# Attention: the division by the sums on GpSimd, the second copy of the turned probabilities on VectorE, four heads ahead, a finished tile's bank released one step later

## The chip, the cores and the metric

The program runs on one core of a Trainium2 chip. The metric is the device time of one execution in microseconds (us); the kernel before has a median of 1674.59 us over 3 runs (1673.91 to 1675.4). Engine names are those of the profile: PE multiplies matrices (PEld loads its weights), DVE is VectorE, ACT is ScalarE, POOL is GpSimd, SP issues most of the DMAs.

## The reference, cut to what matters

Two layers of a backbone over 512 latent tokens and 256 context tokens, width 1024. The change lies in the mixer of layer 0, which puts two groups of heads side by side:

```python
def _softmax_attend(q, k, v):
    s = jnp.einsum('bhgqd,bhkd->bhgqk', q, k, preferred_element_type=jnp.float32) * (ATT_HEAD_DIM ** -0.5)
    p = jax.nn.softmax(s, axis=-1).astype(v.dtype)
    return jnp.einsum('bhgqk,bhkd->bhgqd', p, v)

def _gated_readout(o, og, gain):
    return _merge(_rms(o, gain) * jax.nn.silu(og))

    # in _even_mixer, for the latent tokens
    a_lat = _gated_readout(dirs[0][1] + dirs[1][1], og[:, :, n_ctx:], gla_out_norm)   # 4 gated-linear heads of width 128
    o_blocks = lax.map(lambda qb: _softmax_attend(qb, k_all, va), q_blocks)           # 8 attention heads of width 64
    o_lat = jnp.concatenate([a_lat, b_lat], axis=-1)                                  # then one output projection
```

A latent query reads 768 keys (512 latent, 256 context); a context query reads the 256 context keys.

## The kernel before

**The stage.** `even_mixer` runs generators in a written order (`run("...")`): each letter takes one step of one generator. `x` is `Attention.context()`, `y` is `Attention.latent()`, `t` turns the gated heads into the projection's input (`gated_T`), `r0` and `r1` are the readouts of the two halves of the gated heads, `M` computes modulation columns. While `self.pinned` is set, PE's instructions keep this program order; what the other engines do is put in order by the framework's scheduler, and each engine then executes its own list strictly in that order.

**One latent step.** There are 4 tiles of 128 queries and 8 heads, so 32 pairs (tile, head), numbered i = 0 to 31. Step i of `latent` computes S(i), the scores of pair i (128x768, two banks, tile `S`, two of them in all); DVE takes the row maximum (`amx`, L193), ACT the exponential with its row sum (`prob`, L195), DVE the reciprocal of the sum (`ars`, L196) and the division, as a product of 128x768 in place (L198). The same step then turns an older pair j = i - `ahead` on PE (`turned`: six 128x128 transposes `pT`, four into a bank of the tag `tr`, two into a bank of the tag `sc0` or `sc1`). The four are copied to SBUF by ACT (`probT`, 128x512), the two (128x256) by ACT too, or for every fourth pair by DVE (L210). Of every second step, `values` multiplies two turned pairs with the values (`attO`, 24 small matmuls), and behind the eighth pair of a tile `done` has the result `attO` copied out by ACT (L763) and DVE (L764).

**The bank of the second part.** A tile t of `attO` lives in the bank `sc0` or `sc1` (t % 2). `other()` names the bank in which the two late transposes go: the one that the running tile doesn't hold, or, once that tile is in `self.ended`, the one that it held. Two pairs in succession use the same bank, so the two late transposes of a pair can start only when the copy of the pair before has read it.

**Order in the list of steps.** The latent generator takes its first five steps among those of the context attention; the loop at L1271 takes the rest, with `behind` putting one step of `t`, `r1` or `M` behind some of them. Every fourth pair of a tile (i % 8 = 4) is followed by `queries` for the next tile: four transposes `qT`, read by ACT and by DVE.

**Readout.** `readout(c)` squares (ACT), sums (DVE), takes the power -1/2 (`rstd`, POOL, tile `rs`), multiplies the heads by it (L1233) and by the gate (L1235, with 0.5 where the gate was made by tanh).

Of the kernel before, what the change touches and what calls it, by code (L numbers as in the profile page):

```python
# [17 lines left out]
P = 128  # L18
# [9 lines left out]
EPS = 1e-6  # L28
# [105 lines left out]
class Attention:  # L134
# [43 lines left out]
    def scores(self, t, heads, p):  # L178

        nc, net = self.nc, self.net  # L180
        s = net.mm_tile("S")
        nk = p.shape[-1]
        w = 1024 // len(heads)
        for x, hd in enumerate(heads):
            at = w * x
            for ks in self.k[int(t >= LT)]:
                m = ks[0].shape[-1]
                for i, k in enumerate(ks):
                    net.mm(s[:, at : at + m], self.q[t][:, hd, :], k[:, hd // 4, :], start=(i == 0), stop=(i == 1))
                at += m  # L190
        sv = s.rearrange("p (x k) -> p x k", k=w)[:, :, :nk]
        mx, sm, r = (net.sm.tile([P, len(heads)], F32, tag=tag, name=tag) for tag in (("amx", "asm", "ars") if len(heads) == 1 else ("ms4", "ss4", "rs4")))
        nc.vector.tensor_reduce(mx, sv, axis=AX.X, op=ALU.min)  # L193
        for x in range(len(heads)):
            nc.scalar.activation(p[:, x, :], sv[:, x, :], AF.Exp, bias=mx[:, x : x + 1], scale=-1.0, accum_out=sm[:, x : x + 1])  # L195
        nc.vector.reciprocal(r, sm)  # L196
        for x in range(len(heads)):
            nc.vector.tensor_scalar(p[:, x, :], p[:, x, :], r[:, x : x + 1], None, op0=ALU.mult)  # L198

# [29 lines left out]
                )  # L229

    def done(self, t):
        self.ended.append(t)
        self.net.put(self.cat, slice(4, 8), slice(t * P, (t + 1) * P), self.po[t].rearrange("p (j i) -> p j i", j=4))

    def context(self):
        wp = self.net.wp
        wide = lambda tag, name, dt=F32R: wp.tile([P, WU], dt, tag=tag, bufs=4, name=name)
        kc = wide("wH", "kc").rearrange("p (x n i) -> p x n i", x=2, n=2)
        self.k[1] = [(kc[:, 0], kc[:, 1])]
        ps, pTs = {}, {}  # L240

        def queries(t, tag):
            self.queries(t, wide(tag, f"qs{t}").rearrange("p (h i) -> p h i", h=8))

        def scores(b):
            ps[b] = wp.tile([P, WU], F32, tag="raw", bufs=3, name=f"prob{b}")
            self.scores(LT + b // 2, range(4 * (b % 2), 4 * (b % 2) + 4), ps[b].rearrange("p (x k) -> p x k", x=4))

        def turned(b):
            pTs[b] = wide("wL", f"probT{b}", F32).rearrange("p (c i) -> p c i", c=8)  # L250
            self.turned(ps.pop(b), pTs[b], (1,))

        def values(b):
            pT = pTs.pop(b)
            for j in range(2):
                self.values(LT + b // 2, 2 * (b % 2) + j, [pT[:, 2 * x : 2 * x + 2, :] for x in (2 * j, 2 * j + 1)])

        self.keys(LT, NTT - LT, self.k[1][0])
        queries(LT, "wH")
        yield  # L260
        queries(LT + 1, "wL")
        scores(0)
        yield
        scores(1)
        yield
        turned(0)
        yield
        scores(2)
        values(0)
        yield  # L270
        scores(3)
        turned(1)
        yield
        values(1)
        yield
        self.done(LT)
        turned(2)
        yield
        values(2)
        turned(3)  # L280
        yield
        values(3)
        self.done(LT + 1)

    def latent(self, ap):
        kl = [ap.tile([P, 2, SEQ], F32R, name=f"k{x}") for x in "HL"]
        self.k[0] = [kl] + self.k[1]
        q = lambda t: ap.tile([P, 8, P], F32R, tag="qs", bufs=2, name=f"qs{t}")
        self.keys(0, LT, kl)
        yield  # L290
        self.queries(0, q(0))
        yield

        ahead = 3
        ps, pTs, due = {}, {}, []
        for i in range(8 * LT + ahead + 2):
            t, hd = divmod(i, 8)
            if t < LT:
                ps[i] = ap.tile([P, NT], F32, tag="prob", bufs=4, name="prob")
                self.scores(t, (hd,), ps[i][:, None, :])  # L300
            j = i - ahead
            if 0 <= j < 8 * LT:
                pTs[j] = ap.tile([P, NTT, P], F32, tag="probT", bufs=4, name="probT")
                self.turned(ps.pop(j), pTs[j], (1,) if j % 4 == 3 else (), self.other())
            if due:
                t0, n, xs = due.pop()
                self.values(t0, n, xs)
                if n == 3:
                    self.done(t0)
            if 0 <= j < 8 * LT and j % 2:  # L310
                due.append((j // 8, j // 2 % 4, [pTs.pop(x) for x in (j - 1, j)]))
            if t + 1 < LT and hd == 4:
                self.queries(t + 1, q(t + 1))
            yield


class Net:
# [360 lines left out]
        return gv  # L678


    def rstd(self, ss, n, w=1):
        nc = self.nc
        ms = self.sm.tile([P, w], F32, tag=f"ms{w}", name="ms")
        nc.vector.tensor_scalar(ms, ss, 1.0 / n, EPS, op0=ALU.mult, op1=ALU.add)  # L684
        rs = self.sm.tile([P, w], F32, tag=f"rs{w}", name="rs")
        nc.gpsimd.tensor_tensor(rs, ms, self.neghalf.to_broadcast([P, w]), op=ALU.pow)  # L686
        return rs
# [427 lines left out]
    def even_mixer(self, h, mix, z):  # L1115
# [106 lines left out]
        def readout(c, tiles=tiles):  # L1222

            for t0 in tiles:
                cs = slice(256 * c, 256 * c + 256)
                o = gv[:, t0 : t0 + 2, cs].rearrange("p t (h v) -> p t h v", h=2)
                sq = self.wp.tile([P, WU], F32, tag="mraw", bufs=2, name="sq")[:, :512]
                nc.scalar.activation(sq.rearrange("p (t n) -> p t n", t=2), gv[:, t0 : t0 + 2, cs], AF.Square)
                ss = self.sm.tile([P, 4], F32, tag="ss4", name="ss4")
                nc.vector.tensor_reduce(ss, sq.rearrange("p (x v) -> p x v", v=P), axis=AX.X, op=ALU.add)  # L1230
                rs = self.rstd(ss, P, 4)
                rb = rs.rearrange("p (t h) -> p t h", t=2)[:, :, :, None].to_broadcast([P, 2, 2, P])
                nc.vector.tensor_tensor(o, o, rb, op=ALU.mult)  # L1233
                x = gv[:, t0 : t0 + 2, cs]
                nc.vector.scalar_tensor_tensor(x, x, 0.5 if c else 1.0, og[c][:, t0 : t0 + 2, :], op0=ALU.mult, op1=ALU.mult)  # L1235


        kinds = {
# [28 lines left out]
        with self.pool("att") as ap:  # L1267
            run("y x y g1 x y x y M x y")

            behind = {6: "t", 7: "r1", 9: "t", 10: "r1", 14: "M", 15: "r1", 16: "M", 17: "t", 19: "t", 22: "t", 24: "t", 26: "t", 29: "t"}  # L1270
            for i in range(3, 32 + 5):  # L1271
                run("y " + behind.get(i, ""))
        self.pinned = False
        return cat
# [1010 lines left out]
```

## Time and profile before

| | us |
|---|---|
| median of the runs | 1674.59 |
| the profiled execution | 1675.78 |
| its span | 1674.0 |
| PE busy (share of the span) | 1644.8 (98%) |
| DVE busy | 1311.1 (78%) |
| ACT busy | 916.1 (55%) |
| POOL busy | 129.4 (8%) |

The span is what the trace covers of the profiled execution; 1.8 us lie around it. A matmul's end is modelled, so that in a row the times of matmuls overlap: what PE needed for a group is read from its start to the start of the next one. The latent attention is the stretch from about 250 to 342 us.

### The profile page before, as it was taken

Reading aid. Unit: us, or ns where it says so; the run is one execution under the profiler, and the core shown is the slowest. Engines: PE = TensorE matmul, PEld = TensorE weight load, DVE = VectorE, ACT = ScalarE, POOL = GpSimd, SP = SyncE. Lnnn points to the kernel's source line nnn. Section 1 sums busy time; section 2 is a strip of 40 time slices with the busy share of each in tenths; the row PEclk is TensorE's granted clock in tenths of the full one; section 3 lists DMA queues with packets and bytes.
Section 4 is the critical chain, followed back from the end, with each engine's and each line's share of the span. In section 5 each row is a group of like instructions: output and inputs, shape, how many; then the busy total and the mean of one; then the engine's idle time right before and its main releaser. Section 6 shows DMA issues by size and latency. Waiting matters only on the chain.

```text
span 1674.0 us, 32524 instructions
## 1 busy us (share of the span) xinstructions
PE 1644.8 (98%) x13407; PEld 1481.1 (88%) x13407; DVE 1311.1 (78%) x2097; ACT 916.1 (55%) x1551; POOL 129.4 (8%) x139
## 2 busy tenths in 40 slices
PE   9999999999999999999999999999999999999998
PEld 7899987888999999998887888888888899999886
DVE  5999678976898988777668648788775599987887
ACT  5745567845544443446447436666664565555664
POOL 2004110011000000002102000000000100000310
PEclk9999999999999999999999999999999999999999
DMA  9641012164243445249525541121124333333973
GB/s 336 213 132 41 3 45 86 50 227 160 80 126 114 139 151 176 78 153 205 100 84 193 200 127 57 48 65 40 51 65 150 126 114 115 114 101 102 226 164 138
DMA packets 184736, 204.79 MB, mean 122 GB/s; under 512 B 7142, under 2 KB 141836, under 8 KB 184588
## 3 DMA queue, kind: packets, MB, share of 16 engines
q1 hardware_dynamic: 173996, 181.98, 34.7%
q0 software_dynamic: 9024, 17.30, 5.9%
q10 hardware_dynamic: 1568, 3.43, 0.6%
q8 instruction: 105, 1.72, 0.4%
q14 instruction: 43, 0.35, 0.1%
HBM read 193.23 MB, written 9.46 MB: 121 GB/s over the span
## 4 chain that ended last, share of the span: by engine, by line
PE 83%; DVE 8%; ACT 3%; DMA 3%; issue 2%; POOL 0%; SPq 0%; DVEq 0%; ACTq 0%; POOLq 0%
PE nat L355 12%; PE a L355 10%; PE ff L355 8%; PE E L355 7%; PE oproj L355 6%; PE x L355 6%; PE o L355 5%; PE D L355 4%; PE b L355 3%; PE fq L355 3%; PE gqk L355 2%; PE pearly L355 2%; PE q L355 2%; PE S L355 2%; PE poh L355 1%
## 5 line engine op out<-in xcount | busy, mean ns | idle before, releaser
L355 PE MATMUL nat<-wH,x 128*128 128x256 f32 (+2 forms) x968 | 226.7, 322 | 1.2 <-ACT x L2014 0.6
L860 ACT CAST wH<-raw 128x1024 fp32r<-128x1024 f32 x120 | 124.8, 1051 | 102.7 <-DVE raw L885 40.7
L355 PEld LDWEIGHTS nat<-wH,x 128*128 128x128 f32 x968 | 161.9, 190 | 19.5 <-ACT natq L1196 1.7
L861 DVE TENSOR_TENSOR wL<-raw,wH 128x1024 fp32r<-128x1024 f32 x120 | 145.7, 1222 | 23.6 <-ACT wH L860 23.3
L355 PE MATMUL nat<-wL,x 128*128 128x256 f32 (+2 forms) x484 | 153.5, 317 | 1.8 <-DVE wL L804 1.8
L804 DVE TENSOR_TENSOR wL<-raw,wH 128x1024 fp32r<-128x1024 f32 x79 | 95.8, 1222 | 50.6 <-ACT wH L803 49.8
L355 PE MATMUL ff<-x,wH 128*128 128x512 f32 (+1 forms) x512 | 127.6, 340 | 0.0
L686 POOL TENSOR_TENSOR rs<-ms,neghalf 128x1 f32<-128x1 f32 (+2 forms) x56 | 60.1, 1076 | 777.7 <-DVE ms L684 777.6
L803 ACT CAST wH<-raw 128x1024 fp32r<-128x1024 f32 x79 | 82.2, 1050 | 68.5 <-PE ff L355 19.7
L355 PE MATMUL oproj<-wH,x 128*128 128x512 f32 x320 | 102.2, 394 | 0.4 <-ACT x L1330 0.4
L355 PEld LDWEIGHTS nat<-wL,x 128*128 128x128 f32 x484 | 92.1, 190 | 7.8 <-DVE wL L804 2.7
L615 DVE SCALAR_TENSOR_TENSOR macc<-mraw,scT,macc 128x1024 f32<-128x1024 f32 x70 | 88.0, 1282 | 11.6 <-DMA mraw<-in_mod_w_dram 11.4
L355 PEld LDWEIGHTS ff<-x,wH 128*128 128x128 f32 x512 | 87.3, 190 | 10.0
L355 PE MATMUL x<-wH,two 128*128 128x512 f32 x280 | 90.5, 392 | 0.9 <-DVE y L1851 0.7
L1773 POOL DMA_DIRECT2D t<-in_ffn_w_down_dram x36 | 41.9, 1200 | 640.1 <-DVE t L1812 338.3
L1012 ACT COPY qkh<-arr 128x512 f32<-128x512 f32 x112 | 70.2, 641 | 36.6 <-DVE arr L1017 32.3
L355 PE MATMUL ff<-x,wL 128*128 128x256 f32 (+1 forms) x256 | 86.2, 337 | 0.0
L885 DVE TENSOR_TENSOR raw<-raw 128x512 f32<-128x512 f32 x120 | 82.8, 690 | 2.8
L1017 DVE TENSOR_TENSOR arr<-arr,f 128x512 f32<-128x512 f32 x112 | 74.4, 688 | 2.0 <-ACT qkh L1012 0.3
L355 PEld LDWEIGHTS oproj<-wH,x 128*128 128x128 f32 x320 | 59.9, 188 | 13.0 <-ACT x L1330 1.0
L355 PE MATMUL a<-T,wH 128*128 128x384 f32 (+1 forms) x320 | 70.5, 309 | 0.6 <-ACT qb L923 0.5
L355 PE MATMUL E<-T,wH 128*128 128x384 f32 (+1 forms) x320 | 70.4, 309 | 0.7 <-DVE go L938 0.7
(425 smaller groups left out, 4558.6 us busy)
## 6 DMA issues: line engine op xcount, KB each, us to landing
mraw<-in_mod_w_dram SPq DMA_DIRECT2D x80, 512.0 KB, 4.4
raw<-in_ffn_w_gate_dram SPq DMA_DIRECT2D x44, 512.0 KB, 3.9
raw<-in_ffn_w_up_dram SPq DMA_DIRECT2D x44, 512.0 KB, 4.9
raw<-in_odd_w_in_dram SPq DMA_DIRECT2D x40, 512.0 KB, 3.7
t<-in_ffn_w_down_dram POOLq DMA_DIRECT2D x30, 512.0 KB, 8.3
raw<-in_ffn_w_down_dram SPq DMA_DIRECT2D x28, 512.0 KB, 8.0
mraw<-in_mod_w_dram SPq DMA_DIRECT2D x32, 256.0 KB, 6.3
raw<-in_even_w_in_dram SPq DMA_DIRECT2D x16, 512.0 KB, 5.9
```

The costliest lines, as they stand in the source:

```text
L355: return self.pin(self.nc.tensor.matmul(*a, **k))
L615: nc.vector.scalar_tensor_tensor(a, u, w, a, op0=ALU.mult, op1=ALU.add)
L686: nc.gpsimd.tensor_tensor(rs, ms, self.neghalf.to_broadcast([P, w]), op=ALU.pow)
L803: self.casts = self.casts[-1:] + [nc.scalar.copy(H[:, :m], raw[:, :m])]
L804: vector.tensor_tensor(L[:, :m], raw[:, :m], H[:, :m].bitcast(F32), op=ALU.subtract)
L860: self.nc.scalar.copy(H, f)
L861: self.nc.vector.tensor_tensor(L, f, H.bitcast(F32), op=ALU.subtract)
L885: add = lambda o, x, y: nc.vector.tensor_tensor(o, x, y, op=ALU.add)
L1012: nc.scalar.copy(qkv[:, :, :, half, :], dst)
L1017: nc.vector.tensor_tensor(dst, dst, tb, op=ALU.mult)
L1773: add = lambda o, src: self.pin(nc.gpsimd.dma_start(out=o, in_=src, accum_op=ALU.add))
```

## The change

- The division of one latent pair (L198) goes from DVE, where it is a tensor_scalar, to POOL, as a tensor_tensor with the reciprocal spread over the 768 columns. The context attention, four heads at a time, keeps it on DVE.
- The second copy of the turned probabilities (128x256) is made by DVE for all 32 pairs; before, by DVE for 8 and by ACT for 24.
- `ahead` goes from 3 to 4 and the buffers of `prob` from 4 to 6; the loop takes one step more.
- A finished tile enters `self.ended` only in the step behind the one that finished it, and there only after the transposes. In the context attention `ended` is written where it was.
- `readout(0)`: both products go from DVE to POOL. `readout(1)`: the factor 0.5 moves into `rstd` (`by=4.0`), and the last product becomes a tensor_tensor on DVE.

```diff
@@ scores
         nc.vector.reciprocal(r, sm)
+        if len(heads) == 1:
+            nc.gpsimd.tensor_tensor(p, p, r[:, :, None].to_broadcast([P, 1, nk]), op=ALU.mult)
+            return
         for x in range(len(heads)):
             nc.vector.tensor_scalar(p[:, x, :], p[:, x, :], r[:, x : x + 1], None, op0=ALU.mult)
@@ done / context
     def done(self, t):
-        self.ended.append(t)
...
         self.done(LT)
+        self.ended.append(LT)
...
         self.done(LT + 1)
+        self.ended.append(LT + 1)
@@ latent
-        ahead = 3
-        ps, pTs, due = {}, {}, []
+        ahead = 4
+        ps, pTs, due, over = {}, {}, [], []
...
-                ps[i] = ap.tile([P, NT], F32, tag="prob", bufs=4, name="prob")
+                ps[i] = ap.tile([P, NT], F32, tag="prob", bufs=6, name="prob")
...
-                self.turned(ps.pop(j), pTs[j], (1,) if j % 4 == 3 else (), self.other())
+                self.turned(ps.pop(j), pTs[j], (1,), self.other())
+            self.ended += over
+            over = []
             if due:
                 t0, n, xs = due.pop()
                 self.values(t0, n, xs)
                 if n == 3:
                     self.done(t0)
+                    over = [t0]
@@ rstd
-    def rstd(self, ss, n, w=1):
+    def rstd(self, ss, n, w=1, by=1.0):
...
-        nc.vector.tensor_scalar(ms, ss, 1.0 / n, EPS, op0=ALU.mult, op1=ALU.add)
+        nc.vector.tensor_scalar(ms, ss, by / n, by * EPS, op0=ALU.mult, op1=ALU.add)
@@ readout
-                rs = self.rstd(ss, P, 4)
+                rs = self.rstd(ss, P, 4, 4.0 if c else 1.0)
...
-                nc.vector.tensor_tensor(o, o, rb, op=ALU.mult)
+                e = nc.vector if c else nc.gpsimd
+                e.tensor_tensor(o, o, rb, op=ALU.mult)
...
-                nc.vector.scalar_tensor_tensor(x, x, 0.5 if c else 1.0, og[c][:, t0 : t0 + 2, :], op0=ALU.mult, op1=ALU.mult)
+                e.tensor_tensor(x, x, og[c][:, t0 : t0 + 2, :], op=ALU.mult)
@@ the loop of steps
-            for i in range(3, 32 + 5):
+            for i in range(3, 32 + 6):
```

How the instructions then stand, at three places. **PE at the start of the latent steps**, before, from S(2) on; `S` are the scores (one number each), `pT` the transposes of a pair, `qT` those of the next tile's queries:

```order
L355 MATMUL S_3777<-kH_3598,qs0_3621 128x512
L355 MATMUL S_3777<-kL_3599,qs0_3621 128x512
L355 MATMUL S_3777<-kc_3206,qs0_3621 128x256 x2
L355 MATMUL S_3790<-kH_3598,qs0_3621 128x512
L355 MATMUL S_3790<-kL_3599,qs0_3621 128x512
L355 MATMUL S_3790<-kc_3206,qs0_3621 128x256 x2
L358 MATMUL pT_3803<-ident_74,prob_3701 128x128 x4
L358 MATMUL pT_3809<-ident_74,prob_3701 128x128 x2
L355 MATMUL S_3814<-kH_3598,qs0_3621 128x512
L355 MATMUL S_3814<-kL_3599,qs0_3621 128x512
L355 MATMUL S_3814<-kc_3206,qs0_3621 128x256 x2
```

The same place after:

```order
L362 MATMUL S_3777<-kH_3598,qs0_3621 128x512
L362 MATMUL S_3777<-kL_3599,qs0_3621 128x512
L362 MATMUL S_3777<-kc_3206,qs0_3621 128x256 x2
L362 MATMUL S_3790<-kH_3598,qs0_3621 128x512
L362 MATMUL S_3790<-kL_3599,qs0_3621 128x512
L362 MATMUL S_3790<-kc_3206,qs0_3621 128x256 x2
L362 MATMUL S_3803<-kH_3598,qs0_3621 128x512
L362 MATMUL S_3803<-kL_3599,qs0_3621 128x512
L362 MATMUL S_3803<-kc_3206,qs0_3621 128x256 x2
L365 MATMUL pT_3816<-ident_74,prob_3701 128x128 x4
L365 MATMUL pT_3822<-ident_74,prob_3701 128x128 x2
L365 MATMUL qT_3827<-ident_74,natq_676 128x128 x4
```

Before, the transposes of pair 0 (`pT_3803`) stood between S(3) and S(4) (`S_3814`); after, S(4) (`S_3803`) follows S(3) at once, and `pT_3816`, the transposes of pair 0, stand behind it. From there on each transpose group stands one step later, and `attO` stands behind the even pairs where it stood behind the odd ones.

**DVE at the end of tile 0.** `x` is the copy of the finished bank `attO`, `qs` the reads of the next tile's queries, `amx` a row maximum, `ars` a reciprocal, `probT` a second copy. Before:

```order
L198 TENSOR_SCALAR prob<-prob,ars 128x768
L193 TENSOR_REDUCE amx<-S 128x1
L764 TENSOR_TENSOR x_3685<-attO,x_3684 128x4x128
L196 RECIPROCAL ars<-asm 128x1
L198 TENSOR_SCALAR prob<-prob,ars 128x768
L175 TENSOR_TENSOR qs_4122<-qT,qs_4122 64x512
L193 TENSOR_REDUCE amx<-S 128x1
L175 TENSOR_TENSOR qs_4122<-qT,qs_4122 64x512
L196 RECIPROCAL ars<-asm 128x1
L198 TENSOR_SCALAR prob<-prob,ars 128x768
```

The same place after:

```order
L193 TENSOR_REDUCE amx<-S 128x1
L196 RECIPROCAL ars<-asm 128x1
L213 COPY probT<-pT 128x256
L196 RECIPROCAL ars<-asm 128x1
L771 TENSOR_TENSOR x_3685<-attO,x_3684 128x4x128
L175 TENSOR_TENSOR qs_4111<-qT,qs_4111 64x512
L193 TENSOR_REDUCE amx<-S 128x1
L175 TENSOR_TENSOR qs_4111<-qT,qs_4111 64x512
L213 COPY probT<-pT 128x256
L193 TENSOR_REDUCE amx<-S 128x1
L196 RECIPROCAL ars<-asm 128x1
L213 COPY probT<-pT 128x256
```

The divisions are gone from the list, and the second copy behind the last `qs`, that of pair 9, is queued behind `x`, both `qs` and the maximum between them; `attO` of the pairs 8 and 9 needs it.

**DVE at the late readout** (the third step of `r1`: `wL` is a split of projection weights, `ms`, `gvo<-gvo,rs` and `gvo<-gvo,og` the readout, `modcol` the modulation), before:

```order
L193 TENSOR_REDUCE amx<-S 128x1
L1230 TENSOR_REDUCE ss_4266<-sq 128x4
L804 TENSOR_TENSOR wL<-raw,wH 128x1024
L196 RECIPROCAL ars<-asm 128x1
L684 TENSOR_SCALAR ms<-ss_4266 128x4
L193 TENSOR_REDUCE amx<-S 128x1
L198 TENSOR_SCALAR prob<-prob,ars 128x768
L1233 TENSOR_TENSOR gvo<-gvo,rs 128x2x256
L499 TENSOR_TENSOR modcol_3749<-modT,col 128x8
L1235 SCALAR_TENSOR_TENSOR gvo<-gvo,og_685 128x2x256
```

The same place after, from the maximum of S(16) to the second copy of pair 13:

```order
L193 TENSOR_REDUCE amx<-S 128x1
L196 RECIPROCAL ars<-asm 128x1
L691 TENSOR_SCALAR ms<-ss_4243 128x4
L213 COPY probT<-pT 128x256
L811 TENSOR_TENSOR wL<-raw,wH 128x1024
L1241 TENSOR_TENSOR gvo<-gvo,rs 128x2x256
L196 RECIPROCAL ars<-asm 128x1
L506 TENSOR_TENSOR modcol_3749<-modT,col 128x8
L1243 TENSOR_TENSOR gvo<-gvo,og_685 128x2x256
L506 TENSOR_TENSOR modcol_3749<-modT,col 128x8
L193 TENSOR_REDUCE amx<-S 128x1
L213 COPY probT<-pT 128x256
```

Before, a maximum and a division stood between `ms` and the product that needs POOL's `rs`; after, a copy and the split of the weights, and the next maximum and copy stand behind both products.

POOL's list holds, after, the 16 divisions of the pairs 0 to 15, then the `rs` of this readout, then the other 16 divisions; before, nothing stood ahead of this `rs` but the copies of the keys. SP's list is the same in both kernels.

## Rows read from the trace of the kernel before

**Rows 1.** The page's head: busy time, share of the span and instructions.
```profile
PE 1644.8 (98%) x13407; PEld 1481.1 (88%) x13407; DVE 1311.1 (78%) x2097; ACT 916.1 (55%) x1551; POOL 129.4 (8%) x139
```

**Rows 2.** Stretches: length; PE, PEld, DVE, ACT, POOL busy us (instructions); clock, DMA, GB/s.
```profile
160.00:200.00 40.00, 40.00 (x693) 38.67 (x694) 31.86 (x86) 23.74 (x50) 9.14 (x8) 1.00 0.01 2
...
240.00:280.00 40.00, 36.77 (x333) 30.98 (x332) 34.97 (x65) 27.25 (x63) 4.49 (x6) 1.00 0.35 119
280.00:320.00 40.00, 37.75 (x397) 31.57 (x396) 35.55 (x68) 33.01 (x68) 1.28 (x1) 1.00 0.17 54
320.00:360.00 40.00, 39.21 (x290) 32.44 (x289) 26.75 (x38) 21.71 (x39) 0.00 (x0) 1.00 0.43 145
```

**Rows 3.** Waits from 240 to 352: who waited, for whom, us, times, longest.
```profile
PE pT L358 <- DVE x L764: 2.1, 3, 1.3
```

**Rows 4.** PE in order of time: start, us, instruction; undisturbed steps.
```profile
270.88 0.82 PE L358 MATMUL pT<-ident,prob 128*128 128x128 f32 x6
271.46 0.48 PE L355 MATMUL S<-kH,qs 128*128 128x512 f32 x1
...
272.25 0.82 PE L358 MATMUL pT<-ident,prob 128*128 128x128 f32 x6
272.99 1.53 PE L355 MATMUL attO<-probT,natk 128*64 128x128 f32 x24
274.45 0.65 PE L358 MATMUL catT<-ident,gvo 128*128 128x128 f32 x4
```

**Rows 5.** PE in order of time: first, largest and last stall; a late S.
```profile
256.65 0.50 PE L355 MATMUL S<-kH,qs 128*128 128x512 f32 x1
...
280.51 0.60 PE L358 MATMUL pT<-ident,prob 128*128 128x128 f32 x4
282.41 0.41 PE L358 MATMUL pT<-ident,prob 128*128 128x128 f32 x2 [1.30 <-DVE x L764]
...
326.02 0.48 PE L355 MATMUL S<-kH,qs 128*128 128x512 f32 x1
...
332.43 0.44 PE L358 MATMUL pT<-ident,prob 128*128 128x128 f32 x2 [0.27 <-DVE probT L210]
```

**Rows 6.** DVE: second copy, maximum, reciprocal, division; a maximum behind its scores.
```profile
277.40 0.41 DVE L210 COPY probT<-pT 128x256 f32<-128x256 f32 x1
277.73 0.95 DVE L193 TENSOR_REDUCE amx<-S 128x1 f32<-128x768 f32 x1
278.60 0.16 DVE L196 RECIPROCAL ars<-asm 128x1 f32<-128x1 f32 x1
278.80 0.62 DVE L198 TENSOR_SCALAR prob<-prob,ars 128x768 f32<-128x768 f32 x1
...
327.00 0.96 DVE L193 TENSOR_REDUCE amx<-S 128x1 f32<-128x768 f32 x1 [0.37 <-PE S L355]
```

**Rows 7.** ACT: one exponential, one half of a finished bank's copy.
```profile
258.64 0.90 ACT L195 ACTIVATE prob<-S,amx 128x768 f32<-128x768 f32 x1 [0.50 <-DVE amx L193]
...
280.08 0.62 ACT L763 CAST x<-attO 128x512 fp32r<-128x512 f32 x1
```

**Rows 8.** POOL: products by size, one power.
```profile
18.85 1.41 POOL L804 TENSOR_TENSOR wL<-zraw,wH 128x576 fp32r<-128x576 f32 x1 [5.07 <-ACT wH L803]
...
126.82 1.04 POOL L1382 TENSOR_TENSOR natq<-natq,rs 128x512 f32<-128x512 f32 x1
...
169.43 0.45 POOL L1382 TENSOR_TENSOR natk<-natk,rs 128x128 f32<-128x128 f32 x1
...
295.51 1.28 POOL L686 TENSOR_TENSOR rs<-ms,neghalf 128x4 f32<-128x4 f32 x1 [45.73 <-DVE ms L684]
```

**Rows 9.** DVE: a product beside POOL's at 126.82.
```profile
127.04 1.10 DVE L1017 TENSOR_TENSOR arrg<-arrg,glaf 128x256 f32<-128x256 f32 x1
```

**Rows 10.** DVE at the late readout: split of weights, first product.
```profile
294.01 1.22 DVE L804 TENSOR_TENSOR wL<-raw,wH 128x1024 fp32r<-128x1024 f32 x1
...
296.82 0.69 DVE L1233 TENSOR_TENSOR gvo<-gvo,rs 128x512 f32<-128x512 f32 x1
```

## The prediction

> **What bounds the kernel now.** I read the page's head first, then the stretches, then the waits, then PE in order of time. The reader is to see in the head that PE is busy for 98% of the span and POOL for 8% [rows 1]: a change that leaves PE's work as it is can only take away holes in PE. The stretches say where holes are: none from 160 to 200, 3.23 us (40.00 - 36.77) from 240 to 280, 2.25 from 280 to 320 and 0.79 from 320 to 360 [rows 2]. DVE is busy for 35 of 40 us in the middle two, which makes it the engine that PE waits for there, and the waits name it: the late transposes wait 2.1 us, in three places, for DVE's read of a finished bank [rows 3].
>
> Since matmul ends are modelled, I measure holes by the distance of starts. Where nothing waits, six transposes take 0.58 (270.88 to 271.46), the scores 0.79 (271.46 to 272.25), transposes to values 0.74, `attO` 1.46 (272.99 to 274.45) [rows 4]. A short step is then 0.79 + 0.58 = 1.37, a step with `attO` 0.79 + 0.74 + 1.46 = 2.99, a pair of steps 4.36, so 2.2 a head. Against these distances ten places between S(2) and the last transposes are late, first at 256.65 and last before 332.43: 0.26, 0.66, 0.20, 0.62, 0.50, 1.49, 0.67, 0.69, 0.71, 0.50, together 6.3 us. The largest is to be seen in the rows: from the first four transposes at 280.51 the other two should follow 0.41 later, and start after 1.90 [rows 5]. So 6.3 us is all that the change can take from the latent attention, 0.38% of the whole.
>
> **What goes.** DVE loses 32 divisions of 0.62 (0.54 or so from start to start) and gets 24 copies of 0.41 (0.33 from 277.40 to 277.73) [rows 6]: 32 x 0.54 - 24 x 0.33 = 9.4 us less in some 80. ACT loses the same 24 copies. The bank of a finished tile is no longer taken for the late transposes in the step that finished it, so the three waits of 2.1 us go; with them the 1.49 at 280.51. The two holes of 0.50, the second before 332.43 [rows 5], each a late second copy behind divisions, go too.
>
> **What comes.** Four terms, from the new order on each engine.
>
> Start: S(4) follows S(3) at once, and its bank is that of S(2), which the exponential reads until 258.64 + 0.90 = 259.54 [rows 7]. S(3) is done 2 x 0.8 behind 256.65 plus the 0.26 that stay, at 258.5. So S(4) waits 1.1, and the copy of pair 1, behind a read of `qs`, costs 0.35 more. With the 0.26 this is 1.75, where the first four places now hold 1.74: the deeper pipeline costs at its filling what it saves there.
>
> Tile ends, twice: the copy of an odd pair (9, then 17) stands on DVE behind the bank's read, both `qs` and a maximum. ACT's half of the bank starts 0.38 behind the end of `attO` (279.70 by 280.08) and takes 0.62 [rows 7], so DVE begins at 1.1; three operations of 512 columns at about 0.61 (row 296.82 less the overlap of 0.08) [rows 10], a maximum of 0.87 (277.73 to 278.60) and the copy of 0.33 [rows 6] end at 4.1. PE has until then `qT`, two scores and two groups of transposes, 0.41 + 2 x 0.79 + 2 x 0.58 = 3.2; 0.1 to 0.2 of the rest I give to `qT`'s own lateness. That leaves 0.75 each, 1.5. The third tile end has no `qT` behind it and costs nothing.
>
> Late readout: count from S(15). A maximum starts 0.98 behind its scores (326.02 to 327.00) [rows 5, 6]; that of S(16), 1.37 later, ends at 1.37 + 0.98 + 0.87 = 3.2, and the reciprocal of pair 15 follows it. POOL divides that pair until 3.4 + 1.43 = 4.8. The 1.43 is worked out: POOL's products take 1.04 at 512 columns and 0.45 at 128, 1.54 ns a column, so 1.04 + 256 x 0.00154 [rows 8]; from 1.41 at 576 in proportion it would be 1.88, the upper bound; below the 1.04 of 512 it cannot be. The power `rs` is queued behind it, 1.28 [rows 8], and is there at 6.1; DVE's two products, reciprocal and small ones (1.4), the maximum and the copy of pair 13 end at 8.9. PE asks for that copy in the transposes behind S(18), at 1.37 + 2.99 + 1.6 + 1.2 = 7.1. So 1.9 late. But a row speaks for more: DVE's product of 256 columns took 1.10 beside POOL's product at 126.82 [rows 9], where one of 512 takes 0.69 [rows 10]; it began 0.22 after POOL's and ended only after POOL's 1.04 were over. `wL`, of that kind, stands on DVE while POOL divides, so it or the power is held, by its 1.13 [rows 10], and I take 3.0. The hole of 0.67 there today is contained in the 6.3 that I set against it.
>
> Odd steps: four times `catT` or its copies now follow a short step, where ACT has less time to empty the bank: 0.2 to 0.4 each, 1.0; a guess from the replay of the order, between 0 and 2.
>
> Sum: 1.75 + 1.5 + 3.0 + 1.0 = 7.25 against 6.3, +0.95. The profiled execution, 1675.78, would become 1676.7; it lies 1.2 above the median of 1674.59, so the prediction is 1674.59 + 0.95 = 1675.5.
>
> The POOL term has a rule against it. The Trainium skill (GPSIMD Engine Reference, "Elementwise — side-by-side cycle accounting") gives GpSimd 4497 ns for a product of 2048 fp32 columns, twice VectorE's time; in proportion 768 would take an estimated 1.69, and the sum would be +1.2. The rows here have 1.5 and not 2 times for 512 columns.
>
> **Costed at nothing.** The first readout's six products go to POOL, 1.04 where DVE took 0.69. They lie before the keys' copies, PE has no hole from 160 to 200, and POOL is busy for 9 of 40 us there [rows 2]; if that cover were gone, each 0.35 would reach the context's scores one to one. The factor in `rstd` is the same instruction with other constants; a tensor_tensor for the other form is the same 128x512 pass. Six buffers of `prob` only allow the depth. POOL's 32 products of 1.43 fill 46 us of some 80, at 2.2 us a head: hidden, as each pair has four steps, and from reciprocal to transposes only one product.
>
> **Rivals.**
> *Faster.* My late holes are waits in an order that DVE need not hit: DVE gains 9.4 us of room. If only the filling stays (1.4 of the 1.75), the gain is 6.3 - 1.4 = 4.9: 1669.7. For it speaks that DVE, at 35 of 40 us, is what PE waits for [rows 2, 3]; against it that the holes today sit at places of order, not of load. If only the 1.0 and half of the readout go, it is 1673, within the bound.
> *Slower.* The hold of rows 9 falls on the reciprocals too, which sit ahead of the maxima and copies. In short steps the next reciprocal comes within POOL's product; a mean hold of half a product, 0.7, less the 0.27 of slack in a short step, at 8 of these places, is +3.4, in all +4.4: 1679.0. From a mean hold of 0.57 the result counts as slower. For it speaks 127.04; against it that a reciprocal of one column [rows 6] is not a product of two wide operands. The Trainium skill (SBUF — State Buffer, "SBUF: two separate sides") states that only VectorE operations with two SBUF inputs, or in a two-port mode, share an exclusive lock with GpSimd; row 127.04 agrees, and by that rule this rival falls.
> *POOL becomes the bound.* A product that takes 2.6 instead of 1.43, because of the spread reciprocal, would exceed the 2.2 a head: 32 x 0.4 = 13, 1687. The products in rows 8 of `natq` and `natk` have a spread factor as well, which speaks against it.
>
> **Chances.** What a measurement of this kernel tells from no change is 0.2%, 3.35 us. The forecast and its neighbours within that bound 0.55 (own range 1672.0 to 1677.6); faster rival 0.26; reciprocals held or the worst of my terms (power 1.5, product 1.88, catT 2: +6 at most, 1680.6) 0.16; POOL as the bound 0.03. Faster 0.26, same 0.55, slower 0.19. The range reaches to the faster rival's 1669.7 and past the slower one's 1679.0 only so far as leaves out 2 in 10: 1670.0 to 1679.2.
>
> **What would show it.** POOL's L198 rows at 1.4 to 1.9. S(4) starting near 259.6 with a wait for the exponential. No wait for `x` L771 any more. The second transposes of pair 14 waiting about 3 us for a copy that stands behind L1241 and L1243, and `wL` longer than 1.22 there. `attO` late by 0.75 behind the two tile ends. Reciprocals still 0.16. The prediction is wrong if DVE reaches these copies before PE asks, or if reciprocals take 0.5 and more.

## The result, and the profile after

| | before | after |
|---|---|---|
| median of 20 runs each | 1674.60 us | 1677.80 us |
| lowest to highest | 1673.35 to 1677.21 | 1676.58 to 1680.64 |
| profiled execution | 1675.78 | 1677.57 |
| its span | 1674.0 | 1675.5 |

The ratio is 1.0020, with a 95% interval of 1.0013 to 1.0026: 3.2 us slower, on the edge of the 0.2% that the prediction took for no change. The forecast was +0.95 us, in a range of 1670.0 to 1679.2.

The head of the page and the stretches, to be laid beside [rows 1, 2]; the columns are the same:

```profile
PE 1644.3 (98%) x13407; PEld 1481.6 (88%) x13407; DVE 1303.9 (78%) x2083; ACT 909.8 (54%) x1527; POOL 185.2 (11%) x177
```

```profile
160.00:200.00 40.00, 40.00 (x719) 38.66 (x719) 32.50 (x83) 23.58 (x50) 15.26 (x13) 1.00 0.01 2
240.00:280.00 40.00, 36.06 (x332) 31.14 (x332) 32.09 (x62) 26.10 (x56) 21.15 (x18) 1.00 0.35 119
280.00:320.00 40.00, 35.44 (x359) 29.00 (x356) 30.94 (x57) 27.07 (x52) 20.94 (x15) 0.96 0.17 54
320.00:360.00 40.00, 39.73 (x318) 33.33 (x316) 25.68 (x41) 21.34 (x36) 11.29 (x8) 1.00 0.40 130
```

POOL is busy for 185 us instead of 129 and DVE for 7 us less. In the middle stretches DVE falls from 35 of 40 us to 31 or 32. Yet PE is idle for 3.94 and 4.56 us there, where it was for 3.23 and 2.25: a less loaded DVE did not serve PE sooner. In the stretch from 280 to 320 the granted clock is 0.96, where it was 1.00.

The waits of PE in the latent attention (who waited, for whom, us, times, longest), beside [rows 3]:

```profile
PE attO L362 <- DVE probT L213: 3.7, 3, 1.4
PE pT L365 <- DVE modcol L506: 1.4, 1, 1.4
PE S L362 <- ACT prob L195: 1.1, 1, 1.1
PE pT L365 <- DVE probT L213: 0.8, 3, 0.3
```

The reader is to see that `x` is gone from the list. In its place stand `probT`, `modcol` and an exponential; 1.4 of the 3.7 us for `probT` belong to the context attention and were there before.

By the distances of starts that the prediction used, the holes from S(2) on sum to 9.6 us, against 6.3 before. That is 3.3 more, and the medians differ by 3.2: the loss lies in the latent attention. Directly read, S(1) starts 0.1 us earlier than before and the projection behind the attention (the first pair of `oproj` wH products after the last `attO`) 2.8 later. That delay of 2.8 still stands at 600 us; it is 2.2 at 700, 2.5 at 1000 and 1.5 from 1410 on, so in this pair of executions 1.3 came back in stretches that the change leaves as they were.

PE in order of time: the filling, the first tile end, the late readout. These answer to the stalled rows of [rows 5]:

```profile
259.66 0.47 PE L362 MATMUL S<-kH,qs 128*128 128x512 f32 x1 [1.09 <-ACT prob L195]
...
282.86 0.84 PE L365 MATMUL pT<-ident,prob 128*128 128x128 f32 x6
284.61 1.53 PE L362 MATMUL attO<-probT,natk 128*64 128x128 f32 x24 [0.90 <-DVE probT L213]
...
295.20 0.82 PE L365 MATMUL pT<-ident,prob 128*128 128x128 f32 x6
296.53 0.44 PE L365 MATMUL catT<-ident,gvo 128*128 128x128 f32 x2 [0.51 <-ACT probT L213]
...
297.27 0.40 PE L362 MATMUL S<-kc,qs 128*128 128x256 f32 x2
299.11 0.83 PE L365 MATMUL pT<-ident,prob 128*128 128x128 f32 x4 [1.44 <-DVE modcol L506]
...
300.21 0.69 PE L365 MATMUL pT<-ident,prob 128*128 128x128 f32 x2 [0.27 <-DVE probT L213]
300.83 2.48 PE L362 MATMUL attO<-probT,natk 128*64 128x128 f32 x24
303.24 0.50 PE L362 MATMUL S<-kH,qs 128*128 128x512 f32 x1
```

S(4) waits 1.09 at 259.66. At 284.61 `attO` stands 1.75 behind its transposes instead of 0.74. At the late readout `catT` is 0.68 late, the transposes of pair 14 1.60 and then 0.69 and 0.26, and `attO` takes 2.41 from start to start instead of 1.46.

DVE and POOL at the late readout, against [rows 8, 10], first DVE's rows, then POOL's:

```profile
293.71 0.15 DVE L196 RECIPROCAL ars<-asm 128x1 f32<-128x1 f32 x1
...
294.17 2.38 DVE L811 TENSOR_TENSOR wL<-raw,wH 128x1024 fp32r<-128x1024 f32 x1
297.46 0.69 DVE L1241 TENSOR_TENSOR gvo<-gvo,rs 128x512 f32<-128x512 f32 x1 [0.90 <-POOL rs L693]
...
298.20 0.68 DVE L1243 TENSOR_TENSOR gvo<-gvo,og 128x512 f32<-128x512 f32 x1
298.80 0.16 DVE L506 TENSOR_TENSOR modcol<-modT,col 128x8 f32<-128x8 f32 x1
```

```profile
294.01 1.47 POOL L198 TENSOR_TENSOR prob<-prob,ars 128x768 f32<-128x768 f32 x1 [5.36 <-DVE ms L691]
295.44 1.99 POOL L693 TENSOR_TENSOR rs<-ms,neghalf 128x4 f32<-128x4 f32 x1
```

The split `wL` takes 2.38 where it took 1.22 [rows 10]; it began 0.16 after POOL's product of 1.47. The power `rs` starts only when this product is over, while the split still runs, and takes 1.99, where it took 1.28 [rows 8]. DVE then stands still for 0.90, until `rs` is there, and reads the bank that PE wants next (`modcol`) only at 298.80, behind both products.

The clock around it, in stretches of 2 us (the column behind POOL's instructions is the granted clock):

```profile
296.00:298.00 2.00, 1.16 (x7) 0.85 (x6) 1.10 (x2) 0.95 (x2) 1.43 (x1) 1.00 0.22 33
298.00:300.00 2.00, 0.83 (x4) 0.46 (x4) 2.00 (x7) 0.00 (x0) 1.63 (x1) 0.85 0.63 229
300.00:302.00 2.00, 1.79 (x14) 1.46 (x16) 1.87 (x6) 1.96 (x4) 0.36 (x2) 0.50 0.00 0
302.00:304.00 2.00, 2.00 (x20) 1.74 (x17) 2.00 (x2) 0.52 (x2) 1.32 (x1) 0.80 0.00 0
```

PE is busy for 1.16 and 0.83 of 2 us, and then the granted clock falls to 0.50, the 1.2 GHz level, for the work that PE had been kept from. In finer stretches it is 1.00 up to 299.4, so for the first transposes behind the wait of 1.44, 0.50 from there to 302.5, and 1.00 again from 303 on.

### The profile page after: what moved, and what is told of

It reads as the page before. It is cut to its first block, busy times and chain, and to the rows that moved or that the text cites. A ratio compares the mean times of both kernels' runs of the same rounds, so it can differ in the third digit from the quotient of the medians.

```text
span 1675.5 us, 32655 instructions
## 1 busy us (share of the span) xinstructions
PE 1644.3 (98%) x13407; PEld 1481.6 (88%) x13407; DVE 1303.9 (78%) x2083; ACT 909.8 (54%) x1527; POOL 185.2 (11%) x177
## 4 chain that ended last, share of the span: by engine, by line
PE 84%; DVE 8%; ACT 3%; DMA 3%; issue 1%; POOL 1%; DVEq 0%; SPq 0%; ACTq 0%; POOLq 0%
PE nat L362 12%; PE a L362 10%; PE ff L362 8%; PE E L362 7%; PE x L362 7%; PE oproj L362 6%; PE o L362 5%; PE D L362 4%; PE b L362 4%; PE fq L362 3%; PE gqk L362 2%; PE pearly L362 2%; PE q L362 2%; PE S L362 2%; PE attO L362 2%
```

## The experiments

All ratios are to the kernel before, with 95% intervals; the changed kernel has 1.0020 (1.0013 to 1.0026). The theory was that the loss sits in the order on DVE and POOL at the late readout (with the clock), at the tile ends and in the filling; the chief rivals were DVE's load and the mere presence of POOL's products.

**Three divisions back on DVE.**

```diff
-        if len(heads) == 1:
+        if len(heads) == 1 and 8 * t + heads[0] not in (15, 16, 17):
             nc.gpsimd.tensor_tensor(p, p, r[:, :, None].to_broadcast([P, 1, nk]), op=ALU.mult)
```

> The change, but the division of pairs 15, 16 and 17 stays on DVE (three tensor_scalar of about 0.6 us), so that no POOL product lies ahead of the late readout's power and none beside the two weight splits. Theory (the loss sits at the late readout, in the power queued behind a product, in the split held beside it, and in the clock that falls after the wait): the weight splits take 1.2 us again and not 2.4, the power 1.0 to 1.3, the wait of the transposes for modcol (1.44 us) shrinks to under 0.5, the granted clock stays 1.00 in that stretch, and 2.5 to 3.5 us are gained on the changed kernel: ratio to the kernel before 1.000 (0.9995 to 1.0005). Rival 1 (the pipeline's depth and the tile ends carry the loss): under 1 us gained, ratio 1.0015 to 1.002. Rival 2 (what counts is DVE's load, which grows by 1.6 us here): nothing gained or worse, 1.002 or more.

Measured: 1675.58, ratio 1.0006 (0.9997 to 1.0014), about 2.3 us better than the change. `modcol` is gone from the waits, the clock stays at 1.00, and the power takes 1.01. No split lies beside the readout: the next one comes at 300.68 and takes 1.22 again, the one behind it, with POOL's products back, 1.59:

```profile
PE attO L362 <- DVE probT L213: 4.2, 3, 1.9
```

```profile
300.68 1.22 DVE L811 TENSOR_TENSOR wL<-raw,wH 128x1024 fp32r<-128x1024 f32 x1
...
305.23 1.59 DVE L811 TENSOR_TENSOR wL<-raw,wH 128x1024 fp32r<-128x1024 f32 x1
```

So the late readout is a large part of the loss, but the gain falls a little short of the 2.5 to 3.5 expected: 0.5 went into the second tile end, where `attO` now waits 1.9 instead of 1.4. Since the split moved away together with the product, this run does not say how the gain divides between the queue ahead of the power and the hold of the split.

**All divisions back on DVE.**

```diff
-        if len(heads) == 1:
-            nc.gpsimd.tensor_tensor(p, p, r[:, :, None].to_broadcast([P, 1, nk]), op=ALU.mult)
-            return
```

> The change, but all 32 divisions stay on DVE; the copies on DVE, four steps ahead, the later release and the first readout's products on POOL stay. Theory (POOL's products do harm at the late readout only, and elsewhere they are hidden): the late readout gains about 3 us, 17 us more of DVE's time give back 0.5 to 1.5 us at the tile ends and at second copies: ratio 1.0005 (1.000 to 1.001). Rival (taking the division off DVE is what helps the change, the loss comes from depth and copies): slower than the changed kernel, ratio over 1.0025.

Measured: 1680.49, ratio 1.0036 (1.0023 to 1.005). The theory missed and the rival's number came: with 24 more copies on DVE its 32 divisions are too much.

```profile
PE attO L359 <- DVE probT L210: 5.0, 3, 2.4
PE pT L362 <- DVE probT L210: 2.4, 4, 1.5
```

```profile
312.00:314.00 2.00, 0.56 (x6) 0.56 (x8) 1.94 (x4) 1.08 (x3) 0.00 (x0) 0.77 0.15 59
314.00:316.00 2.00, 2.00 (x22) 1.87 (x18) 1.93 (x7) 0.99 (x2) 0.00 (x0) 0.50 0.00 0
```

The longest waits are now for DVE's `probT`. One of them, 2.42 before an `attO` at 313.44, is followed by a granted clock of 0.50 as well.

**Three steps ahead.**

```diff
-        ahead = 4
+        ahead = 3
...
-            for i in range(3, 32 + 6):
+            for i in range(3, 32 + 5):
```

> The change with heads three steps ahead and the loop one step shorter (six buffers stay). Theory (the filling of the deeper pipeline costs about 1.4 us at S(4), and POOL's product of 1.47 us fits in three steps): the wait of 1.1 us of S(4) for an exponential is gone, the late readout still waits, ratio 1.001 (1.0005 to 1.0015). Rival (the depth is needed once POOL lies between reciprocal and transposes): transposes wait for POOL in the trace, ratio 1.002 or more.

Measured: 1676.05, ratio 1.0007 (0.9998 to 1.0016). The wait of S(4) is gone, and so are the long waits of `attO` at the tile ends (with three ahead `attO` stands behind odd steps again); the late readout waits 2.2 for a second copy, in one piece (2.16 before the transposes at 296.79), and the granted clock stays at 1.00 behind it. Both theories have a part: one group of transposes, at the tail, does wait for POOL.

```profile
PE pT L365 <- DVE probT L213: 2.9, 4, 2.2
...
PE pT L365 <- POOL prob L198: 1.1, 1, 1.1
```

**Four steps ahead, alone.** To the kernel before, only this:

```diff
-        ahead = 3
+        ahead = 4
...
-                ps[i] = ap.tile([P, NT], F32, tag="prob", bufs=4, name="prob")
+                ps[i] = ap.tile([P, NT], F32, tag="prob", bufs=6, name="prob")
...
-            for i in range(3, 32 + 5):
+            for i in range(3, 32 + 6):
```

> The kernel before with one edit: four steps ahead, six buffers, one step more. Theory (the filling costs the wait of 1.1 us of S(4) and what follows it, about 1.4, and attO behind even steps meets DVE's queues at the tile ends): ratio 1.0015 (1.001 to 1.0025). Rival (depth hides waits elsewhere and pays its filling back): ratio 1.000 or less.

Measured: 1678.23, ratio 1.0019 (1.0011 to 1.0028), 3.6 us: on its own the depth costs as much as the whole change. The filling shows twice, in S(4), which waits 1.1 for an exponential, and in a second copy that is late on ACT (1.2), and two of the three waits for `x` are there as before:

```profile
PE pT L358 <- DVE x L764: 1.8, 2, 1.3
PE pT L358 <- ACT probT L210: 1.5, 2, 1.2
```

By the distances of starts the filling holds 3.6 us here (1.7 before) and the places behind it 6.0 (4.5). The second part of the theory is not borne out: no `attO` waits at a tile end in this trace.

**Later release, alone,** in the kernel before:

```diff
     def done(self, t):
-        self.ended.append(t)
...
+            self.ended += over
+            over = []
             if due:
...
                     self.done(t0)
+                    over = [t0]
```

> The kernel before with one edit: a finished tile's bank is released one step later. Theory (the three waits of the late transposes for DVE's read of a finished bank, 2.1 us in all, are on the path): the waits for x vanish and 1.5 to 2.1 us are gained, ratio 0.9988 (0.9985 to 0.9992). Rival (DVE is as late as before, and the next wait in its queue, for qs or a second copy, takes their place): the waits for x vanish, others grow, ratio 1.000 (0.9995 to 1.0005).

Measured: 1672.93, ratio 0.9989 (0.9980 to 0.9998), 2.1 us faster than the kernel before, which had 1675.05 beside it. Of the 2.1 us of waits for `x` [rows 3], 0.3 is left, at the context's end:

```profile
PE pT L362 <- DVE x L768: 0.3, 1, 0.3
```

**Release at once, in the change** (the same edit taken out of it):

> The change, but a finished tile's bank is released in the step that finished it, as before. Theory (the later release takes three waits of 2.1 us away, in the change as well as alone): transposes wait for x again behind the tile ends, 1 to 2.5 us slower than the changed kernel, ratio 1.003 (1.0025 to 1.0035). Rival (with the divisions off DVE the read of the bank comes in time, and the later release is worth nothing): ratio 1.002 or less.

Measured: 1679.57, ratio 1.0026 (1.0016 to 1.0036), slower than the change by 1.7 us by the medians and by 1.0 by the ratios; the intervals overlap, so the sign is likely and the size open. The wait is not the expected one: `x` comes nearly in time (0.2), and the transposes wait for the second copy of the pair before in the same bank, 1.1 and 1.3 at two tile ends:

```profile
PE pT L361 <- DVE probT L213: 3.5, 5, 1.3
```

**Division on POOL, alone,** in the kernel before:

```diff
         nc.vector.reciprocal(r, sm)
+        if len(heads) == 1:
+            nc.gpsimd.tensor_tensor(p, p, r[:, :, None].to_broadcast([P, 1, nk]), op=ALU.mult)
+            return
```

> The kernel before with one edit: the division of the 32 latent pairs on POOL; three steps ahead, copies and release as before. Theory (POOL's products hold up the late readout by the queue in front of the power, 1 to 2 us, and the last transposes by 1.1; the room on DVE makes the three reads of finished banks earlier by 0.5 to 1.5 in all): ratio 1.0005 (1.0000 to 1.001). Rival (DVE's load is what PE waits for, so 17 us less on DVE gain 2 us or more): ratio 0.9988 or less.

Measured: 1675.10, ratio 1.0001 (0.9992 to 1.0010). DVE is 32 x 0.54 = 17 us freer, and in sum nothing comes of it. By the distances of starts the late readout holds 2.1 us (0.7 before), where PE now waits 0.7 for `modcol` and 0.8 for a copy, and all other places 4.5 (5.5 before). So the room on DVE gave back about 1.0, and POOL's queue at the readout took 1.4, the latter as expected (of the 1.1 expected at the last transposes, 0.3 came). The wait for `x` is shorter by 0.3 only, since `x` waits for its place in the order:

```profile
PE pT L361 <- DVE x L767: 1.8, 3, 1.3
```

**Copies back on ACT, in the change.**

```diff
-                self.turned(ps.pop(j), pTs[j], (1,), self.other())
+                self.turned(ps.pop(j), pTs[j], (1,) if j % 4 == 3 else (), self.other())
```

> The change, but 24 of the 32 second copies stay on ACT as before. Theory (at the two tile ends attO waits because the second copy is queued on DVE behind the bank's read, two qs and a maximum): the two waits of 0.9 and 1.4 us of attO for DVE's probT fall to under 0.5 together, some holes of 0.5 to 0.7 behind ACT's copies come back as before the change, the late readout stays; ratio 1.001 (1.0005 to 1.0015). Rival (the copies on DVE help, since ACT's copies are what PE waited for before): slower than the changed kernel, 1.0025 or more.

Measured: 1675.87, ratio 1.0010 (1.0001 to 1.0019), 1.9 us better than the change. The waits of `attO` at the two tile ends shrink from 0.9 and 1.4 to one of 0.6, and one copy at the filling is now late on ACT (1.2):

```profile
PE attO L362 <- ACT probT L213: 0.6, 1, 0.6
...
PE pT L365 <- ACT probT L213: 1.3, 2, 1.2
```

The late readout stays, with the hold the other way round: the split starts first (294.12) and takes 1.22, and POOL's product behind it (294.29) takes 2.38; `modcol` is waited for about as long as in the change.

**Queries two steps earlier, in the change.**

```diff
-            if t + 1 < LT and hd == 4:
+            if t + 1 < LT and hd == 2:
```

> The change, but the next tile's queries are turned two steps earlier, at the third head of a tile instead of the fifth, so that their reads no longer stand on DVE behind the finished bank's read. Theory (the queue on DVE at the tile ends): the waits of attO for probT of 0.9 and 1.4 us go below 0.6 together, 1.5 to 2 us gained, ratio 1.001 (1.0005 to 1.0015). Rival (attO waits there for the copy's own source or for DVE's load, not for the queue of reads): the waits move with the reads or stay, ratio 1.002.

Measured: 1677.43, ratio 1.0017 (1.0008 to 1.0026). At the tile ends the theory holds: no `attO` is more than 0.4 late there. But the reads for tile 1 now meet the filling, and S(5) waits 1.35 for an exponential behind them, after the 1.0 of S(4):

```profile
PE S L362 <- ACT prob L195: 2.4, 2, 1.3
```

The gain at one place was spent at another; the time alone would have spoken for the rival.

**First readout back on DVE, in the change.**

```diff
-                e = nc.vector if c else nc.gpsimd
+                e = nc.vector
```

> The change, but the first readout's six products stay on DVE (as tensor_tensor). Theory (they lie in a stretch where PE has no holes, so where they run does not matter): same time as the changed kernel, ratio 1.002 (1.0014 to 1.0025), PE busy 40.00 of 40 from 160 to 200 in both. Rival (POOL's products there hold up the keys' copies or DVE): 0.5 to 2 us faster than the changed kernel, ratio 1.001 or less.

Measured: 1678.16, ratio 1.0020 (1.0011 to 1.0029). No effect, as the full PE from 160 to 200 said.

**A faster version.** Three steps ahead, as above, and five divisions on DVE:

```diff
-        if len(heads) == 1:
+        if len(heads) == 1 and 8 * t + heads[0] not in (15, 16, 17, 30, 31):
```

> The change with three steps ahead and the divisions of pairs 15, 16, 17, 30 and 31 on DVE. Theory (filling, late readout and the tail, where the last transposes waited 1.1 us for POOL with three ahead, are what costs): the wait of 2.2 us for a second copy at the late readout goes to under 0.5 and the wait for POOL vanishes; about 3 us are gained on three ahead alone, ratio 0.9988 (0.998 to 0.9995), faster than the kernel before. Rival (three us more on DVE come back as other waits): ratio 1.0000 or more.

Measured: 1672.90, ratio 0.9989 (0.9980 to 0.9998). The time is as expected and POOL is gone from the waits; but at the late readout 1.1 stays, where under 0.5 was expected:

```profile
PE pT L365 <- DVE probT L213: 1.8, 4, 1.1
```

That copy, of pair 13, is queued on DVE behind the product that needs `rs`. Sent to ACT:

```diff
-                self.turned(ps.pop(j), pTs[j], (1,), self.other())
+                self.turned(ps.pop(j), pTs[j], () if j == 13 else (1,), self.other())
```

> Three steps ahead, the divisions of pairs 15, 16, 17, 30 and 31 on DVE, and the second copy of pair 13 on ACT, the rest as in the change. Theory (what is left at the late readout is the second copy of pair 13, queued on DVE behind the product that needs the power, for which the transposes still waited 1.1 us): that wait goes below 0.3, 0.8 to 1.2 us gained on the kernel with the five divisions alone, ratio 0.9983 (0.9975 to 0.9990). Rival (ACT is as late there): same as that kernel, 0.9989.

Measured: 1672.05, ratio 0.9985 (0.9976 to 0.9994), the fastest of all, 2.6 us under the kernel before.

```profile
PE pT L365 <- DVE probT L213: 0.7, 3, 0.3
```

The wait of 1.1 is gone from `probT`, and one step later a hole of 0.3 has grown to 0.9 (0.3 of it a wait for an exponential); the gain on the version above, 0.9 us by the medians, is within both intervals.

## Why the prediction came near, and where it was short

**The sign and the places were right, the size was not**: +0.95 forecast, +3.2 measured, inside a range that also held a gain of 4.6. By the prediction's own terms, holes after against those predicted: filling 0.25 + 1.25 + 0.18 + 0.51 = 2.2 for 1.75; tile ends 1.0 + 1.5 = 2.55 for 1.5; late readout 1.60 + 0.69 + 0.26 + 0.95 = 3.5 for 3.0; `catT` behind a short step 0.68, at one place, for 1.0 at four; the rest 0.7, among it a late second copy at 322.36, for nothing. Together 9.6 for 7.25, and the 2.35 between them is what the forecast lacks. It lies in the tile ends (1.05), the filling (0.45), the late readout (0.5, and that by two errors that nearly cancel) and the rest (0.7), less 0.3 at `catT`.

*Late readout: the mechanism held, one term was missing, and the size came near by luck.* The queue of `rs` behind pair 15's division and the hold of `wL` are in the rows after (2.38 for 1.22), and with three divisions back on DVE 2.3 us come back. The forecast let the split or the power be held; both were, the split until the product was over and then the power until the split was (1.99, against 1.01 with no split beside it). The forecast had a second copy late by 3.0; in fact the bank of `modT` was late first, with `modcol` behind the second product, and both waits cost 1.60 + 0.69 = 2.3. The other 1.2 is the fall of the clock, which the sum did not have: it makes the last transposes 0.26 and `attO` 0.95 longer. Of the five traces with a wait of 1.4 for `modcol` (the change, the copies on ACT, the queries earlier, the first readout on DVE, the release at once) all five show a granted clock of 0.50 behind it. That the wait brings the fall is argued from this and not shown: no run filled the wait with other work and kept the rest, and the wait of 2.16 with three ahead, longer but alone, has no fall behind it.

*Tile ends: 2.55 for 1.5.* The chain was the one predicted (`x`, `qs`, maximum, `qs`, copy):

```profile
280.98 0.69 DVE L771 TENSOR_TENSOR x<-attO,x 128x512 fp32r<-128x512 f32 x1 [0.39 <-ACT x L770]
281.70 0.68 DVE L175 TENSOR_TENSOR qs<-qT,qs 64x512 fp32r<-64x512 f32 x1
282.42 0.96 DVE L193 TENSOR_REDUCE amx<-S 128x1 f32<-128x768 f32 x1
283.41 0.69 DVE L175 TENSOR_TENSOR qs<-qT,qs 64x512 fp32r<-64x512 f32 x1
284.13 0.42 DVE L213 COPY probT<-pT 128x256 f32<-128x256 f32 x1
```

It ends at 284.55, 3.57 behind the start of `x`. The forecast had DVE begin 1.1 behind the end of `attO` (280.25) and end at 4.1; it began at 0.7, since ACT's half started sooner than 0.38, and ended at 4.3, since the five follow one another without the overlap that the sum took off (3.57 for 3.0). PE's own part took 3.35, the 3.2 and the 0.15 of the forecast, but the 0.15 is not a lateness of `qT`: the last transposes stand 0.74 and not 0.58 ahead of `attO`. At the second tile end the same five end 4.8 behind `attO` (308.04 to 312.87), because ACT has an exponential of 0.91 (from 307.80) in front of its half of the bank:

```profile
280.36 0.59 ACT L770 CAST x<-attO 128x512 fp32r<-128x512 f32 x1
...
308.69 0.58 ACT L770 CAST x<-attO 128x512 fp32r<-128x512 f32 x1
```

That half starts 0.11 and 0.65 behind `attO`: a wait on another engine that the forecast took from one place, the 0.38 of [rows 7], as if it held for both. Moving the queries away emptied both places (no `attO` more than 0.4 late), which shows that the queue is the cause.

*What goes.* The waits for `x` went, and alone the later release is worth 2.1 us: right. In the change it is worth 1.0 to 1.7, not clear of noise, and without it the late transposes wait for a second copy and not for `x`. What was not seen is that the deeper pipeline is the dear part. "Costs at its filling what it saves there" holds to 0.45 us in the change, but four steps ahead cost 3.6 us alone, half of it at the filling, and taking them out of the change gives 2.2 back by the ratios. The waits of `attO` at the tile ends need both the depth and the copies on DVE: they are not there with the depth alone, with three ahead they go, and with the copies on ACT they shrink to 0.6.

*Faster rival: falls.* That room on DVE would dissolve the waits is refuted by the division alone, which frees DVE by 17 us and has the ratio 1.0001: outside the late readout it gave back 1.0 of 5.5 us, not the 4.9 of the rival.

*Slower rival: falls.* Reciprocals stay at 0.15 to 0.17 us throughout. Held were VectorE operations with two operands from SBUF, as row 294.17 after shows, and not only wide ones. `aff`, of 16 columns, takes 0.17 in the kernel before; beside a product of POOL it ends when the product ends, in the change (first pair of rows) and with the copies on ACT (second pair):

```profile
305.58 0.53 DVE L653 SCALAR_TENSOR_TENSOR aff<-modcol,col 128x16 f32<-128x16 f32 x1
...
304.61 1.47 POOL L198 TENSOR_TENSOR prob<-prob,ars 128x768 f32<-128x768 f32 x1 [1.30 <-DVE ars L196]
```

```profile
305.39 1.40 DVE L653 SCALAR_TENSOR_TENSOR aff<-modcol,col 128x16 f32<-128x16 f32 x1
...
305.30 1.47 POOL L198 TENSOR_TENSOR prob<-prob,ars 128x768 f32<-128x768 f32 x1 [1.49 <-PE catT L365]
```

So the prediction's reason, that a reciprocal is not a product of two wide operands, is right in the operands and wrong in the width. The Trainium skill (SBUF — State Buffer, "SBUF: two separate sides") says that a VectorE operation with two SBUF inputs and a GpSimd operation that reads SBUF lock each other out for a whole instruction, whichever starts first; these rows agree. *POOL as the bound: falls*; a product takes 1.47 where nothing holds it (1.84 and 2.38 where a VectorE product does), by the rows' slope 1.43. The estimate of 1.69, in proportion to the Trainium skill's figure (GPSIMD Engine Reference, "Elementwise — side-by-side cycle accounting"), which is for an add of 2048 columns, was too high.

*Costed at nothing:* the first readout on POOL, confirmed. The form of the second readout's last product cost nothing either (0.68 for 0.69). POOL's product between reciprocal and transposes was hidden with four ahead; with three it showed, 1.1 at the tail.

*The parts together.* Alone: release -2.1, division +0.4, depth +3.6, in sum +1.9. The change is +3.2, and the first readout is worth nothing, so the copies and what the parts do to each other would make the other 1.3; the copies taken out give 1.9 back. Each of these figures carries 1 to 1.5 us of noise by its interval, so the 1.3 is not shown to differ from nothing, and how it would divide is open: the copies were not run alone.

## What to carry to other kernels

Unloading an engine that others wait for helps only if the instruction waited for stands behind the work that goes; read its place in the engine's list, not the engine's load. An elementwise operation moved to GpSimd brings its own queue: look for each small operation that lives there (here a power), and at VectorE operations with two operands in SBUF, narrow ones too, that will run beside it. Each wait that a change adds is to be laid beside the next ones in time: in the five traces here where a wait of 0.5 and one of 1.4 stood within three us, a fall of the clock followed, which in the change cost 1.2 more.

## What was not expected of the hardware

After PE had been idle for 0.51 us before 296.53 and 1.44 before 299.11, the granted clock was 0.50 from 299.4 to 302.5 and back at 1.00 by 303; the third idle time, 0.27 before 300.21, lies already in the slow part. A single wait of 1.91 (three divisions on DVE) or 2.16 (three ahead) left it at 1.00, one of 2.42 (all on DVE) was followed by 0.50. So the length of one wait does not tell in these traces whether the clock falls, and what does is open. A VectorE operation of 16 columns took 1.40 beside a POOL product, and POOL's product 2.38 beside a VectorE one that began 0.17 earlier. And the power of four columns on POOL took 1.99 beside a wide VectorE product, where it takes 1.01 to 1.50 at the first readout in the same trace.
